# The order of the weights' loads, and the queue of some other transfers, in a hybrid decoder layer on one core

## The chip, the core and the metric

The kernel runs on one core of one Trainium2 chip. The core has engines that each work through their own list of instructions in order: TensorE (PE, with its weight loads shown apart as PEld), VectorE (DVE), ScalarE (ACT), GpSimd (POOL) and SyncE (SP). SP computes nothing here; it issues transfers between the chip's main memory and the core's own memory. ACT and POOL can issue transfers too, POOL as one of its ordinary instructions. The transfers of all of them are carried by the same 16 DMA engines. The metric is the device time of one execution in microseconds (us); a lower one is better.

## The reference

One inference step of a one-layer decoder is computed in float32, for a prompt of 2048 tokens and for a small batch of 8 samples with 4 tokens each. With the model width 1024:

```python
xn  = rms_norm(x, norm_mix_pre)
qk, v_m, o_m, gates, q_a, k_a, v_a = split(xn @ w_in)         # 1024 x 2312
c_new, h = mlstm(short_conv(qk), v_m, gates)                  # 4 heads, chunks of 128 tokens
att      = windowed_attention(q_a, k_a, v_a, sinks)           # 8 heads, window 128
y_m = sigmoid(o_m) * rms_norm(h, mlstm_norm);  y_a = rms_norm(att, attn_norm)
x = x + rms_norm([y_m, y_a] @ w_out, norm_mix_post)           # 1024 x 1024
u = rms_norm(x, norm_ffn_pre)
x = x + rms_norm(relu(u @ w_up)**2 @ w_down, norm_ffn_post)   # 1024 x 4096 x 1024
x = x + sigmoid(x @ w_pgate) * (p @ w_pproj)                  # 1024 x 1024 and 256 x 1024
```

The mLSTM head group keeps a running maximum `m` along the tokens (the stabiliser of its exponentials), so the weights of a chunk of 128 tokens are `exp(log_d - m_t)`, where `m_t` is one maximum for each head and token. Outputs are the tokens' `x` and the new states of both head groups.

## The kernel before

**Tiling and stages.** The prompt is cut into 16 blocks of 128 tokens. A first stage (`project`, called once for each of six chunks of two or three blocks) does the norm, the input projection and, interleaved with it, the mLSTM recurrence (`mlstm_chunk`) and the windowed attention (`swa_chunk`). The small batch goes with the last chunk. Both head groups write their results to a scratch tensor in main memory, `yd`, two halves of 512 columns for each block. Then three groups of two chunks go, one after another, through the output projection (`mix_load`, `mix_mm`, `mix_post`), the MLP (`mlp`, 16 steps of 256 hidden columns, of which the first two are plain and the others build the product `u @ w_up` from seven smaller ones) and the gated embedding (`gate_post`, `gate_embed`, `gate_mm`).

**Precision.** Each weight matrix piece is split into two parts, a rounded high part and the remainder, and each product is made of three matmuls (`mm3`). So a weight that is used for the first time is loaded as it is (a tile `wr`, or `wb` for the blocks of `w_up`), copied to the high part by ACT (line 254), and the remainder is made on POOL or DVE (line 255). The pair (a tile `w`, 528 KB or less) is then also stored to a scratch tensor `wk` in main memory, and later chunks load the finished pair from there.

**The ring of weights** (`Ring`). There are five raw tiles and seven pair tiles (`RAWS, PAIRS`, line 75), used in turn. A list (`plan`) gives the weights in the order in which TensorE uses them, and `take` makes the next one where the program reaches it: `get` takes a pair tile, stores an earlier pair that is due (`store`, line 282, on POOL), and either loads the kept pair (line 289) or calls the maker, which loads the raw weight and splits it. Raw loads stand in `product` (line 307, the `wb` blocks), `row` (351), `heads` (363), `multi` (374) and `pairs` (385). All of them are issued by `dma`, which is SP's queue; `put` is POOL's queue:

```python
dma, put = nc.sync.dma_start, nc.gpsimd.dma_start
here = tc.keep_in_program_order
```

**What sets the order.** The program text is not the order in which an engine gets its instructions. A planner in the framework lets a clock of its own run with estimated durations, and gives each engine the next instruction that by this clock is ready, so an instruction with nothing to wait for can be placed far ahead of its place in the text. On the chip each engine then keeps the planned order and waits at an instruction until its inputs are there. `here(ins)` takes away the planner's freedom for one instruction: it is placed behind the instruction that was written before it on the same engine, whichever that was. TensorE's instructions are all kept in the order of the text (class `Flow`). Of SP's transfers none is; of POOL's, the stores of pairs (line 282) and one store of the decode stage are.

**The other transfers on SP's queue** are the input blocks `x` (line 477), constants, the broadcast of the running maxima to all partitions (`weights` in `mlstm_chunk`, line 961, tile `Wt`, one for each of the 16 blocks; ACT stores the maxima to the scratch tensor `mbd` in line 906, and DVE adds a mask to `Wt` in line 962, an instruction that is kept in the order of the text), the two halves of `yd` for the output projection (`load_y`, line 848), the two post-norm weight vectors (`gain`, line 1453, tiles `gpost` and `gffn`, which use one buffer in turn), the rows of `p` (lines 1875 and 1877) and the last six stores of the output (`finish`, line 1833, where `last` is true for the chunk of blocks 14 and 15 and the small batch; each has two halves of 512 columns). All other output stores of line 1833 go over POOL.

Of the kernel before, what the change touches and what calls it, by code (L numbers as in the profile page):

```python
# [11 lines left out]
U32 = mybir.dt.uint32  # L12
# [6 lines left out]
P = 128  # L19
D = 1024  # L20
# [10 lines left out]
AD = 64  # L31
# [91 lines left out]
def bc(ap, axis, n):  # L123
    v = ap.unsqueeze(axis)
    shape = list(v.shape)
    shape[axis] = n
    return v.broadcast_to(tuple(shape))
# [71 lines left out]
def hybrid_layer(ctx: ExitStack, tc: tile.TileContext, A, O):  # L199
# [4 lines left out]
    dma, put = nc.sync.dma_start, nc.gpsimd.dma_start  # L204
    here = tc.keep_in_program_order
# [47 lines left out]
    def wsplit(hi, lo, src, eng=None):  # L253
        act.copy(hi, src)  # L254
        ins = (eng or weng()).tensor_tensor(lo, src, hi.bitcast(F32), ALU.subtract)  # L255
        if pinned:
            here(ins)

    class Ring:


# [22 lines left out]
        def get(self, key, n, make):  # L284

            t = self.tile(n)
            self.store()
            if key in self.kept:
                dma(t.bitcast(U32), self.kept[key])
            else:  # L290
                make(t[:, 0], t[:, 1])
                if self.uses[key] > 1:
                    self.keep(key, t)
            return t[:, 0], t[:, 1]
# [4 lines left out]
        def product(self, key, i, src):  # L299


            def make(h, l):
                if i == 0:
                    self.blocks = []
                    for e in range(2):
                        t = self.wide.tile([P, KT // 2, 2 * P], F32, tag="w", name=f"{self.nm}b{self.n}{e}")
                        dma(t, src[e * 512 : (e + 1) * 512].rearrange("(k p) n -> p k n", p=P))
                        self.blocks += [t[:, :, :P], t[:, :, P:]]
                a11, a21, a12, a22 = self.blocks
                eng = iter([dve if e == "d" else pool for e in UENG[i]])  # L310
                h, l = [v.rearrange("p (k n) -> p k n", k=4) for v in (h, l)]
                if i == 2:
                    next(eng).tensor_tensor(a21, a21, a22, ALU.add)
                    next(eng).tensor_tensor(a11, a21, a11, ALU.subtract)
                elif i == 3:
                    self.last = self.tile(512)
                    wsplit(*[self.last[:, e].rearrange("p (k n) -> p k n", k=4) for e in range(2)], a22, next(eng))
                    next(eng).tensor_tensor(a22, a22, a11, ALU.subtract)
                elif i == 6:
                    next(eng).tensor_tensor(a12, a12, a11, ALU.subtract)  # L320
                wsplit(h, l, (a11, a12, a11, a22, None, a21, a12)[i], next(eng))

            if i == 4 and key not in self.kept:
                t = self.last
                if self.uses[key] > 1:
                    self.keep(key, t)
                v = t[:, 0], t[:, 1]
            else:
                v = self.get(key, 512, make)
            return [t.rearrange("p (k n) -> p k n", k=4) for t in v]  # L330
# [17 lines left out]
        def row(self, key, src, n):  # L348
            def make(h, l):
                raw = self.load(n)  # L350
                dma(raw, src)
                wsplit(h, l, raw)

            return self.get(key, n, make)

        def heads(self, key, src, j, n):


            def make(h, l):
                raw = self.load(n)  # L360
                for s in range(2):
                    o = s * 256 + j * AD
                    dma(raw[s * AD : (s + 1) * AD], src[o : o + AD])
                wsplit(h, l, raw)

            return self.get(key, n, make)

        def multi(self, key, srcs, kn, n):
            three = lambda v: v.rearrange("p (k n) -> p k n", k=kn)

            def make(h, l):
                raw = self.load(kn * n)
                for off, w, s in srcs:
                    dma(three(raw)[:, :, off : off + w], s)
                wsplit(h, l, raw)

            return [three(v) for v in self.get(key, kn * n, make)]

        def pairs(self, key, segs):


            def make(h, l):
                raw = self.load(512)
                for s, src in enumerate(segs):
                    dma(raw.rearrange("p (k s n) -> p k s n", k=2, s=2)[:, :, s], src)
                v = raw.rearrange("p (k s j c) -> p k j s c", k=2, s=2, j=2)
                h, l = (t.rearrange("p (k j s c) -> p k j s c", k=2, j=2, s=2) for t in (h, l))
                for k in range(2):
                    wsplit(h[:, k], l[:, k], v[:, k])

            return [v.rearrange("p (k n) -> p k n", k=2) for v in self.get(key, 512, make)]
# [451 lines left out]
    def load_y(pool_, tag, b):  # L843

        src = yds if b == "s" else yd[b]
        t = pool_.tile([P, D], F32, tag=tag, name=f"y_{b}")
        for e in range(2):
            dma(t[: src[e].shape[0], e * 512 : e * 512 + 512], src[e])
        return t

    def mix_heads(x, i, b, t, banks=ps_m):
# [100 lines left out]
    def mlstm_chunk(r, blocks):  # L952
# [5 lines left out]

        def weights(i):
            Wt = sm.tile([P, MH, P], F32, tag="Wt", name=f"Wt{blocks[i]}")  # L960
            dma(Wt, bc(r["mbd"][:, i * P : (i + 1) * P], 0, P))
            here(dve.tensor_tensor(Wt, Wt, bc(mask, 1, MH), ALU.add))
            for h in range(MH):
                act.activation(Wt[:, h], Wt[:, h], AF.Exp, bias=cq(i, 0, h), scale=-1.0)
            Ws[i] = Wt
# [12 lines left out]
        for i, b in enumerate(blocks):  # L978
# [15 lines left out]
            Wt = Ws.pop(i)  # L994
# [40 lines left out]
        while todo:  # L1035
            finish()
            yield 0.5
# [412 lines left out]

    def gain(src, nm):
        g = gp.tile([P, D], F32, tag="g", name=nm)
        dma(g, src[0:1, :].broadcast_to((P, D)))
        return g

    gpost, gffn = gain(A["norm_mix_post"], "gpost0"), None
# [41 lines left out]
    f, yt, ut, xt = {}, {}, {}, {}  # L1498
# [126 lines left out]

    def mlp(gi, chunks, sample):
        nonlocal gffn
        gffn = gain(A["norm_ffn_post"], f"gffn{gi}")
        G = f"{gi}"
        if sample:  # L1630
            f["t"] = es2.enter_context(tc.tile_pool(name="ft", bufs=1, reuse_waits="tile")).tile(
# [3 lines left out]
        def up(s, ci, wu, hid):  # L1635
            c = chunks[ci]
            W = len(c) * P + (HS if sample else 0)
            x = ut[ci]
            for ft in range(FS):
                nm = f"{G}{s}{ci}{ft}"  # L1640
                fs_ = slice(ft * P, (ft + 1) * P)
                ps = psum(ps_mm, "up" + nm)
                for k in range(KT):
                    w = [t[:, k % 2, fs_] for t in wu[k // 2]]
                    mm3(ps[:, :W], w, x.at(k, slice(0, W)), k == 0, k == KT - 1)
                    pe.tick()
                t = wp.tile([P, UW], F32, tag="re", name="re" + nm)[:, :W]
                hidden(s, ci, ft, t, ps[:, :W], hid)
                pe.tick()
# [131 lines left out]
        def down_weights():  # L1781
            return [[t[:, :512] for t in w] for w in ring.take(FS)]
# [3 lines left out]
        for ci in range(2):  # L1786
            if ci == 1:
                pe.drain(tsp)
                pe.drain(dec)
                es_lp.close()  # L1790
                es_t = ExitStack()
                tp = es_t.enter_context(tc.tile_pool(name="tp", bufs=1, side="right", reuse_waits="tile"))
                ring.wide = es_t.enter_context(tc.tile_pool(name="wide", bufs=WIDE, side="right", reuse_waits="tile"))
                tsp.add(sums())
            for s in range(FAST):
                if ci == 0:
                    hids.append({})
                up(s, ci, ring.take(4), hids[s])
            for s in range(FAST):
                for half in range(2):  # L1800
                    down(s, ci, half, down_weights(), hids[s])
# [23 lines left out]
    def finish(b, half, pg, pv, n, nm, last):  # L1825
        hs = slice(half * 512, half * 512 + 512)
        t = gw.tile([P, 512], F32, tag="sg", name=f"sg{nm}{half}")
        act.activation(t[:n], pg, AF.Tanh, scale=0.5)
        dve.scalar_tensor_tensor(t[:n], t[:n], 1.0, pv, ALU.add, ALU.mult)
        o = gw.tile([P, 512], F32, tag="ot", name=f"ot{nm}{half}")  # L1830
        dve.scalar_tensor_tensor(o[:n], t[:n], 0.5, f[b][:n, hs], ALU.mult, ALU.add)
        dst = y_s[:, hs] if b == "s" else y_p[b * P : (b + 1) * P, hs]
        (dma if last else put)(dst, o[:n])

    def gate_post(gi, ci, c, sample):

# [168 lines left out]
```

## Time and profile before

| | |
|---|---|
| time, median of 3 runs | 2611.17 us (2611.08 to 2614.02) |
| the profiled execution, its own time | 2623.78 us |
| its span, from the first instruction to the last | 2621.7 us |
| mean granted TensorE clock in it | 0.989 of full speed |
| busy: PE, DVE, ACT, POOL | 2534.7, 1483.0, 974.3, 620.3 us |
| transfers: SP's queue (q1), POOL's queue (q0) | 474.02 MB, 174.54 MB |

The profile is of one execution, and that execution took 12.61 us more than the median of the runs. A row of the timeline or of the chain of waits begins with the start in us from the first instruction and the duration. An `SPq` row is an issue of a transfer by SP's queue; where several are merged into one row, the duration goes from the start of the first to the end of the last, waits between them included. Square brackets give the idle time of the engine just before the instruction and what ended it. A row of the list of waits reads: who waited, for whom, the sum in us, how many times, the longest. A row of the list of issues gives the count, the size and the median time from the issue to the landing. A row by stretch of time gives, for PE, PEld, DVE, ACT and POOL, the busy time and the number of instructions, and then the granted clock, the share of the DMA engines that was busy, and GB/s.

### The profile page before, as it was taken

The numbers are of one execution on the slowest core, as the hardware profiler recorded it, in microseconds if no ns is written. First come the engines' busy times: TensorE is split into PE (matmuls) and PEld (weight loads), VectorE is DVE, ScalarE is ACT, GpSimd is POOL, SyncE is SP. The second block draws the span as 40 slices with busy tenths as digits, with TensorE's granted clock in tenths as the row PEclk, the third lists the DMA queues.
The fourth block names the chain that finished last, engine by engine and source line by source line (L and its number), as shares of the span: only waits on it lengthen the run. The fifth ranks groups of instructions, "written<-read, shape, count | busy, mean of one in ns | idle before, by whom it ended". The sixth has DMA issues, their size and how long they took to land.

```text
span 2621.7 us, 39337 instructions
## 1 busy us (share of the span) xinstructions
PE 2534.7 (97%) x14260; PEld 2204.3 (84%) x14260; DVE 1483.0 (57%) x3162; ACT 974.3 (37%) x2167; POOL 620.3 (24%) x988
## 2 busy tenths in 40 slices
PE   7999999998999999999999999999999999999998
PEld 7787888777778888888877788999998879999986
DVE  6666656665657655656744654444446346444553
ACT  5545444544445444444523342222223134222231
POOL 5311111112433666666523200000001011000010
PEclk9999999999999999999999999999999999999999
DMA  9756656576898666666799765555556899777787
GB/s 315 273 192 201 207 181 213 194 244 227 260 343 287 254 250 253 244 254 251 271 341 318 255 201 188 188 191 188 187 187 233 295 334 359 253 255 256 256 299 235
DMA packets 220433, 651.10 MB, mean 248 GB/s; under 512 B 25397, under 2 KB 59401, under 8 KB 220224
## 3 DMA queue, kind: packets, MB, share of 16 engines
q1 hardware_dynamic: 170032, 474.02, 53.4%
q0 software_dynamic: 50160, 174.54, 17.3%
q8 instruction: 113, 1.85, 0.3%
q14 instruction: 80, 0.66, 0.1%
q10 hardware_dynamic: 48, 0.03, 0.0%
HBM read 494.34 MB, written 155.25 MB: 248 GB/s over the span
## 4 chain that ended last, share of the span: by engine, by line
PE 77%; DVE 8%; DMA 7%; issue 3%; ACT 2%; POOL 2%; SPq 0%; ACTq 0%; DVEq 0%; POOLq 0%
PE up L148 21%; PE dn L148 21%; PE mo L148 5%; PE pg L148 5%; PE v L148 3%; DMA w<-wk 3%; PE o L148 3%; DMA wk<-w 2%; PE qk L148 2%; PE qa L148 2%; PE gv L148 2%; DVE hl L232 2%; PE aT L152 1%; PE aO L148 1%; PE pv L148 1%
## 5 line engine op out<-in xcount | busy, mean ns | idle before, releaser
L148 PE MATMUL dn<-w,hh 128*128 128x512 f32 x1792 | 564.0, 396 | 6.3 <-ACT re L1654 3.8
L1759 DVE TENSOR_TENSOR f<-f,dn 128x512 f32<-128x512 f32 x420 | 286.9, 686 | 220.5 <-PE dn L148 218.4
L148 PEld LDWEIGHTS dn<-w,hh 128*128 128x128 f32 x1792 | 334.2, 189 | 84.7 <-DVE f L1759 6.8
L148 PE MATMUL dn<-w,hl 128*128 128x512 f32 x896 | 354.5, 396 | 1.6 <-DVE hl L232 1.6
L1734 DVE TENSOR_TENSOR re<-up,re 128x384 f32<-128x384 f32 (+1 forms) x294 | 151.9, 517 | 320.2 <-PE up L148 320.2
L148 PEld LDWEIGHTS dn<-w,hl 128*128 128x128 f32 x896 | 168.8, 188 | 43.5 <-DVE hl L232 5.1
L1735 ACT COPY re<-up 128x384 f32<-128x384 f32 (+1 forms) x42 | 18.8, 448 | 392.0 <-PE up L148 392.0
L1654 ACT ACTIVATE re<-re 128x384 f32<-128x384 f32 (+1 forms) x168 | 83.0, 494 | 207.5 <-DVE re L1734 203.9
L232 DVE TENSOR_TENSOR hl<-re,hh 128x384 fp32r<-128x384 f32 (+1 forms) x192 | 137.6, 717 | 16.8 <-ACT hh L231 15.7
L282 POOL DMA_DIRECT2D wk<-w x242 | 134.1, 556 | 34.4 <-DVE w L255 25.2
L254 ACT CAST w<-wr 128x512 fp32r<-128x512 f32 (+2 forms) x152 | 88.9, 597 | 95.9 <-PE up L148 32.3
L254 ACT CAST w<-wb 128x512 fp32r<-128x512 f32 x98 | 60.6, 620 | 168.4 <-PE dn L148 114.6
L255 POOL TENSOR_TENSOR w<-wr,w 128x512 fp32r<-128x512 f32 (+2 forms) x76 | 100.2, 1319 | 80.5 <-ACT w L254 79.5
L255 POOL TENSOR_TENSOR w<-wb,w 128x512 fp32r<-128x512 f32 x70 | 92.3, 1319 | 110.3 <-ACT w L254 109.8
L1460 POOL DMA_DIRECT2D x<-x1d x16 | 8.7, 545 | 463.5 <-PE up L148 449.4
L1655 ACT ACTIVATE re<-re 128x384 f32<-128x384 f32 (+1 forms) x192 | 94.9, 494 | 5.9
L231 ACT CAST hh<-re 128x384 fp32r<-128x384 f32 (+1 forms) x192 | 92.6, 482 | 8.3
L1067 ACT ACTIVATE s<-s,swt 128x257 f32<-128x257 f32 (+1 forms) x128 | 63.3, 496 | 65.8 <-DVE swt L1064 65.8
L1061 DVE CUSTOM_DVE_ANT_0 s<-aS,cst,sink 128x256 f32<-128x256 f32 (+1 forms) x128 | 57.1, 472 | 52.0 <-PE aS L148 51.6
L148 PE MATMUL up<-t2h,w 128*128 128x384 f32 (+1 forms) x336 | 85.1, 320 | 0.0
L148 PE MATMUL up<-t0h,w 128*128 128x384 f32 (+1 forms) x336 | 85.1, 320 | 0.0
L148 PE MATMUL up<-t1h,w 128*128 128x384 f32 (+1 forms) x336 | 85.1, 320 | 0.0
(1526 smaller groups left out, 6415.7 us busy)
## 6 DMA issues: line engine op xcount, KB each, us to landing
w<-wk SPq DMA_DIRECT2D x728, 512.0 KB, 4.9
wk<-w POOLq DMA_DIRECT2D x238, 512.0 KB, 7.2
wr<-in_w_down_dram SPq DMA_DIRECT2D x64, 256.0 KB, 8.2
wb<-in_w_up_dram SPq DMA_DIRECT2D x28, 512.0 KB, 6.9
w<-wk SPq DMA_DIRECT2D x20, 528.0 KB, 3.9
x<-in_x_prompt_dram SPq DMA_DIRECT2D x16, 512.0 KB, 4.4
y<-yd SPq DMA_DIRECT2D x32, 256.0 KB, 7.0
xr<-in_x_prompt_dram POOLq DMA_DIRECT2D x16, 512.0 KB, 9.4
```

Source lines behind the costliest of these rows:

```text
L148: ins = self.pe.matmul(out, lhsT, rhs, start=start, stop=stop)
L231: act.copy(hi, src)
L232: dve.tensor_tensor(lo, src, hi.bitcast(F32), ALU.subtract)
L254: act.copy(hi, src)
L255: ins = (eng or weng()).tensor_tensor(lo, src, hi.bitcast(F32), ALU.subtract)
L282: here(put(self.kept[key], t.bitcast(U32)))
L1061: dve.tensor_tensor_reduce(s_[:, s, lo : 2 * P], pS[:, s, lo:], bias[:, j, lo:], 1.0 if s == 0 else 0.0625, sink[:, h : h + 1], ALU.add, A ...
L1067: act.activation(e_, e_, AF.Exp, bias=nm[:, s : s + 1], accum_out=sm[:, s : s + 1])
L1654: act.activation(t, src, AF.Relu)
L1655: act.square(t, t)
L1734: add = lambda out, a, b: dve.tensor_tensor(out, a, b, ALU.add)
L1759: dve.tensor_tensor(out(i), out(i), ps, ALU.add)
```

## The change

A helper `wload` is added that issues a load on SP's queue and keeps it in the order of the text. All loads of weights (kept pairs and the five kinds of raw loads) use it. Five kinds of other transfers change in queue or place: the broadcast of the maxima, the two halves of `yd` and the post-norm weights go over POOL's queue; the `gffn` vector is loaded later in `mlp`, where the second chunk's part begins, instead of at its start; and of the last six stores the three of the first half go over POOL's queue, so that SP keeps three.

```diff
+    def wload(out, src):
+
+        here(dma(out, src))
+
...
             if key in self.kept:
-                dma(t.bitcast(U32), self.kept[key])
+                wload(t.bitcast(U32), self.kept[key])
...
-                        dma(t, src[e * 512 : (e + 1) * 512].rearrange("(k p) n -> p k n", p=P))
+                        wload(t, src[e * 512 : (e + 1) * 512].rearrange("(k p) n -> p k n", p=P))
...
-                dma(raw, src)
+                wload(raw, src)
...
-                    dma(raw[s * AD : (s + 1) * AD], src[o : o + AD])
+                    wload(raw[s * AD : (s + 1) * AD], src[o : o + AD])
...
-                    dma(three(raw)[:, :, off : off + w], s)
+                    wload(three(raw)[:, :, off : off + w], s)
...
-                    dma(raw.rearrange("p (k s n) -> p k s n", k=2, s=2)[:, :, s], src)
+                    wload(raw.rearrange("p (k s n) -> p k s n", k=2, s=2)[:, :, s], src)
...
         for e in range(2):
-            dma(t[: src[e].shape[0], e * 512 : e * 512 + 512], src[e])
+            put(t[: src[e].shape[0], e * 512 : e * 512 + 512], src[e])
...
             Wt = sm.tile([P, MH, P], F32, tag="Wt", name=f"Wt{blocks[i]}")
-            dma(Wt, bc(r["mbd"][:, i * P : (i + 1) * P], 0, P))
+            put(Wt, bc(r["mbd"][:, i * P : (i + 1) * P], 0, P))
...
         g = gp.tile([P, D], F32, tag="g", name=nm)
-        dma(g, src[0:1, :].broadcast_to((P, D)))
+        put(g, src[0:1, :].broadcast_to((P, D)))
...
     def mlp(gi, chunks, sample):
         nonlocal gffn
-        gffn = gain(A["norm_ffn_post"], f"gffn{gi}")
...
             if ci == 1:
                 pe.drain(tsp)
+                gffn = gain(A["norm_ffn_post"], f"gffn{gi}")
                 pe.drain(dec)
...
-        (dma if last else put)(dst, o[:n])
+        (dma if last and half == 1 else put)(dst, o[:n])
```

## The prediction

> **What bounds the kernel now.** I read the page's busy times first, then the list of waits of PE, then that of SP's queue, and then the timelines where the two meet.
>
> ```profile
> span 2621.7 us, 39337 instructions
> PE 2534.7 (97%) x14260; PEld 2204.3 (84%) x14260; DVE 1483.0 (57%) x3162; ACT 974.3 (37%) x2167; POOL 620.3 (24%) x988
> ```
>
> PE bounds it. The change takes no matmul away, so all it can win is PE's idle time, 2621.7 - 2534.7 = 87.0 us, and what idle time costs afterwards in clock. Of PE's waits, these name a kept weight (`w<-wk`), and one more will turn out to be for one:
>
> ```profile
> PE mo L148 <- DMA w<-wk: 5.5, 3, 2.8
> PE qk L148 <- DMA w<-wk: 4.5, 3, 3.9
> PE pg L148 <- DMA w<-wk: 1.8, 1, 1.8
> PE up L148 <- DMA w<-wk: 1.6, 1, 1.6
> ```
>
> That is 13.4 us, and with 3.7 us more (in Part 2) 17.1: 0.7% of the span is about the whole prize. On SP's queue the waits that stand ahead of weights without being about them are these (the second row is of the stretch 690 to 760 us, as is the third; the others are of the whole run):
>
> ```profile
> SPq L961 <- DMA mbd<-Mt: 33.1, 6, 7.0
> SPq L374 <- DVE w L255: 11.3, 1, 11.3
> SPq L289 <- DMA wk<-w: 6.6, 1, 6.6
> SPq L1833 <- DVE ot L1831: 12.6, 3, 10.9
> ```
>
> Most of these waits hurt nobody, because the ring holds seven pairs. The sum is made only where one of them meets a wait of PE.
>
> **Part 1: the maxima leave SP's queue.** In the last chunk SP came to line 961 after its weights, ACT had only then issued the store of the maxima, and SP stood until it landed. The weights behind it came late:
>
> ```profile
> 586.81 14.64 SPq L289 DMA_DIRECT2D w<-wk  x8
> 608.20 0.92 SPq L961 DMA_DIRECT2D Wt<-mbd  x2
> 609.22 30.63 SPq L289 DMA_DIRECT2D w<-wk  x13
> ...
> 602.43 0.25 ACTq L906 DMA_DIRECT2D mbd<-Mt  x1
> ...
> 614.84 0.58 PE L148 MATMUL qk<-x5h,w 128*128 128x256 f32 x1 [3.91 <-DMA w<-wk]
> ...
> 612.90:619.70 6.80, 4.86 (x23) 4.86 (x24) 1.81 (x4) 0.80 (x2) 0.18 (x1) 0.50 0.66 267
> ```
>
> SP stood from 586.81 + 14.64 = 601.45 to 608.20. PE lost 3.91 us, and then ran 4.86 busy us at a clock of 0.50, of which half, 2.43 us, is a loss: 6.3 us together. The load that PE waited for is the next one on SP, so with that wait gone it is issued up to 6.75 us earlier, more than PE's 3.91. The wait goes to POOL, and there it has room: POOL sat idle at just that time,
>
> ```profile
> 609.46 0.50 POOL L616 DMA_DIRECT2D zsd<-qa1se  x1 [8.17 <-DVE qa1se L570]
> ```
>
> so behind it stand a small store and copies that nobody wants soon. In the other places PE waited 4.5 - 3.9 = 0.6 us for `qk`'s weights, and I count that at the end. **Gain 6.3 us**, between 3.9 (if the clock falls for another reason) and 6.3.
>
> **Part 2: loads keep their turn.** At the change from the output projection to the MLP the planner had put raw loads of `w_up` (line 374) ahead of kept weights that PE needs sooner. Their raw tiles were not free, and SP stood:
>
> ```profile
> 701.00 14.38 SPq L374 DMA_DIRECT2D wr<-in_w_up_dram  x4
> 715.48 9.64 SPq L289 DMA_DIRECT2D w<-wk  x5
> ...
> 726.92 1.19 PE L148 MATMUL mo<-w,yt01h 128*128 128x512 f32 x2 [3.73 <-DVE ms L1490]
> ...
> 725.50:732.30 6.80, 5.38 (x13) 4.13 (x14) 4.54 (x11) 1.15 (x2) 4.41 (x9) 0.50 1.02 408
> ```
>
> For the kept weight issued at 715.48 the list of issues of that moment alone gives its time to landing, and so it does for the pair's store issued at 710.88:
>
> ```profile
> w<-wk SPq DMA_DIRECT2D x1, 512.0 KB, 11.3
> ...
> wk<-w POOLq DMA_DIRECT2D x1, 512.0 KB, 12.1
> ```
>
> 715.48 + 11.3 = 726.8, which is when PE went on: the page names DVE, but the weight ended this wait. Full price: 3.73 and half of 5.38, 6.4 us. But PE needs the second weight at once too, and its load waited the 6.6 us quoted above for a store of the pair that held its place in the ring, 710.88 + 12.1 = 723.0. That wait is POOL's and not SP's order; with it alone, and a load that then takes 5 us, PE would stand to about 728 again. The store took 12.1 us while DMA was full, partly of the 4 x 256 KB put ahead, which at the 408 GB/s of that stretch are 2.6 us. So the bounds are 0 and 6.4 and I take the row of those 2.6 us, rounded down: **gain 2 us**. The raw loads of `w_up` now start later, behind sixteen kept ones; three of the eight did so before with no wait of PE, so nothing for that. In the long stage of fresh `wb` blocks the order changes too (SP had them two steps ahead, now one). A step lasts 913.17 - 881.13 = 32.0 us, which covers a landing of 6.9 us:
>
> ```profile
> 881.13 2.74 SPq L307 DMA_DIRECT2D wb<-in_w_up_dram  x2
> ...
> 913.17 2.74 SPq L307 DMA_DIRECT2D wb<-in_w_up_dram  x2
> ...
> wb<-in_w_up_dram SPq DMA_DIRECT2D x28, 512.0 KB, 6.9
> ```
>
> **Part 3: the post-norm weights.** In the last group SP stood at `gffn` until DVE had done with `gpost`, with PE's next weight behind it:
>
> ```profile
> 2169.60 0.33 SPq L1453 DMA_DIRECT2D gffn<-in_norm_ffn_post_dram  x1
> 2170.02 3.97 SPq L289 DMA_DIRECT2D w<-wk  x5
> ...
> 2176.73 0.39 PE L148 MATMUL up<-ut20h,w 128*128 128x272 f32 x1 [1.57 <-DMA w<-wk]
> ```
>
> **Gain 1.6 us** (0 to 1.6: the DMA engines are full here). In its new place `gffn` is wanted only in the last of the sixteen steps of `mlp`.
>
> **Part 4: the halves of `yd` and the last stores.** 34 loads and three stores leave SP. No wait of PE stands behind them, also not behind the 10.9 us that SP waited for the last `ot`: **0**.
>
> **What POOL pays.** 16 + 34 + 6 + 3 = 59 more transfers, each as the 28 of line 1833:
>
> ```profile
> L1833 POOL DMA_DIRECT2D out_dram<-ot x28 | 15.3, 545 | 153.2 <-DVE ot L1831 153.2
> ...
> 661.61 0.53 POOL L616 DMA_DIRECT2D zsd<-vse  x1 [11.77 <-DVE vse L570]
> ...
> SPq L289 <- DMA wk<-w: 21.6, 7, 8.0
> ```
>
> 59 x 0.545 = 32 us, on an engine that is busy 24%. It is on the path in two places at most. Ahead of the output projection six halves and `gpost` (7 x 0.545 = 3.8 us) come before splits and stores of the first `w_out`; POOL had 11.77 idle us there. In the gated embedding of the first group six halves and `gpost` stand among stores of `w_pgate`, whose landing SP awaits in the stretch 1330 to 1365 us (the third row); PE's 1.8 us for `pg` are there. 0 to 3.8 each; I take 1 us each since POOL has gaps in both: **cost 2 us**.
>
> Sum: 6.3 + 2 + 1.6 - 2 = 7.9 us, made against the profiled 2623.78 (2615.9 then); the same off the median, 2611.17 - 7.9 = 2603.3, and with the 0.6 us of Part 1 **2602.7 us**.
>
> The Trainium skill, DMA: Bandwidth & Descriptors, section Issuing engines are not separate DMA queues, says that transfers of all issuers share the same 16 engines, and that spreading them saves only the issuer's time. By it alone the change would win nothing but SP's issue time, which is hidden. The trace has in 601.45 to 608.20 what that sentence leaves out, a wait of one issuer that holds back unrelated transfers; I give its outcome a chance below, as the second rival.
>
> **The rivals.**
>
> *All waits at SP's hand go.* If the stores in Part 2 land sooner as well, the full 6.4 counts, and the 1.99 us at 741 with the half-clock stretch behind it:
>
> ```profile
> 741.54 0.73 PE L148 MATMUL mo<-w,yt01h 128*128 128x512 f32 x2 [1.99 <-DMA w<-wk]
> ...
> 742.60:746.00 3.40, 3.40 (x13) 2.81 (x12) 0.28 (x2) 0.00 (x0) 0.00 (x0) 0.50 1.03 420
> ```
>
> 6.9 + 6.4 + 1.99 + 1.70 + 1.6 = 18.6 with no cost on POOL: 2592.6 us. Against it: the ring's stores are still POOL's.
>
> *Nothing is won.* PE's weights are held by the ring's stores and by full DMA engines (`wk<-w` 21.6 us in 35 us of the gate stage, share 1.02), POOL's extra 32 us makes those stores later by as much as SP gains; and where unkept loads of `x` or `p` stand between, a weight is kept behind those and not behind the last weight, so the turn holds only in part. 2611 us.
>
> *Slower: `Wt` comes too late over POOL.* DVE's mask addition (line 962) is kept in its place, so DVE, and PE behind it, stand if `Wt` is late. The loads of a third block have little time: one took 8.6 us and DVE waited, another was issued 10.6 us ahead:
>
> ```profile
> 118.36 1.20 SPq L961 DMA_DIRECT2D Wt<-mbd  x1
> 126.97 0.69 DVE L962 TENSOR_TENSOR Wt<-Wt,cst 128x512 f32<-128x512 f32 x1 [2.67 <-DMA Wt<-mbd]
> ...
> 239.82 0.37 SPq L961 DMA_DIRECT2D Wt<-mbd  x1
> 250.39 0.68 DVE L962 TENSOR_TENSOR Wt<-Wt,cst 128x512 f32<-128x512 f32 x1
> ...
> Wt<-mbd SPq DMA_DIRECT2D x16, 256.0 KB, 4.2
> POOL hist L768 <- ACT u L767: 101.6, 24, 11.5
> ```
>
> 10.6 - 4.2 = 6.4 us are free; it decides when POOL's queue delays `Wt` by more. POOL's longest wait in this stage, 11.5, would do it, by 5.1 us, in the third blocks of chunks 0 to 3: four times, 20.4 us, less the 7.9: 2623.7 us. Against it: the median wait in that row is about 101.6 / 24 = 4.2.
>
> The Trainium skill, SBUF — State Buffer, section SBUF: two separate sides, speaks against this change as well: a transfer from GpSimd can wait until a DVE copy gives back a port that GpSimd needs to write the descriptors, and it tells of 3100 ns in place of 620. By it `Wt` would come some 2.5 us later, an estimate from that page, which the 6.4 us cover, and the sum stays.
>
> **How the numbers follow.** 0.42 for the forecast (2597 to 2608 in itself), 0.20 for the larger gain, 0.23 for nothing won, 0.15 for slower. A measurement tells 0.2%, 5.2 us, from no change: under 2605.9 is faster, over 2616.4 slower. Faster: 0.42 x 0.85 + 0.20 + 0.04 = 0.60; slower 0.15 and 0.03 of the third case: 0.18; the rest 0.22. The range goes from below the larger gain to most of the slower case: 2588 to 2619.
>
> **What would show it.** Part 1: SP goes on with weights at 601 us, and neither the 3.91 nor the half clock after it is there. Part 2: no line 374 ahead of the kept `w_out` pairs, and the wait before `mo` is under 3.7 us but not zero. Part 3: no 1.57 us at the start of the last `up`. POOL busy about 652 us. The forecast is wrong if DVE waits for `Wt` in line 962 for more than 10 us, if ACT's or SP's waits for `wk<-w` grow, or if the planner, given a new order on SP and POOL, moves work of DVE and ACT so that PE waits in places that this text doesn't name.

## The result, and the profile after

The kernel after took 2629.73 us (median of 4 runs, 2623.86 to 2632.42) against 2612.6 for the kernel before on the same chip: ratio 1.0063, 95% interval 1.0050 to 1.0075, about 16 us slower. The forecast was 2602.7, faster; the range went to 2619. **The direction was wrong.**

The page after, first its busy times, then rows of the list of PE's waits:

```profile
span 2630.6 us, 39303 instructions
PE 2534.9 (96%) x14260; PEld 2202.7 (84%) x14260; DVE 1476.7 (56%) x3162; ACT 973.8 (37%) x2167; POOL 651.2 (25%) x1047
```

```profile
PE mo L148 <- DMA w<-wk: 8.9, 7, 4.6
...
PE dn L148 <- ACT re L1657: 4.2, 1, 4.2
PE ut100t L152 <- DVE g L238: 3.3, 1, 3.3
PE yt5t L152 <- DVE g L238: 2.9, 1, 2.9
PE xt20t L152 <- DVE xt00l L232: 2.6, 1, 2.6
...
PE pg L148 <- DMA w<-wk: 2.2, 1, 2.2
PE up L148 <- DMA w<-wk: 1.3, 2, 1.1
PE qk L148 <- DMA w<-wk: 1.0, 2, 0.8
```

PE's work is the same; only its idle time grew. POOL's 651.2 us are the 31 us more that were forecast. Of the waits for kept weights, that of `qk` fell from 4.5 to 1.0 us; `up` has 1.3 instead of 1.6, `pg` 2.2 instead of 1.8, and `mo` 8.9 instead of 5.5, or instead of 9.2 if the 3.73 us that were for a weight, though labelled DVE, are counted with it. Of the waits for DVE shown here, `ut100t` had 1.5 us before, `yt5t` 1.1 and `xt20t` 0.8. The wait of `dn` for ACT's relu (`re`) moved: before had one too, of nearly the same size, but in the first MLP, where the kernel after has none. The row of the list, and of the timeline, before:

```profile
PE dn L148 <- ACT re L1654: 3.8, 1, 3.8
...
795.52 1.22 PE L148 MATMUL dn<-w,hh 128*128 128x512 f32 x2 [3.83 <-ACT re L1654]
```

The lines of the kernel after are 3 or 4 higher than those of before (the relu of `hidden` is L1654 before and L1657 after), and every load kept in turn now has line 261.

Where the two profiled executions part is seen from the start of the same matmul or transpose in both timelines (us from the start, rounded; the differences are of the times as recorded):

| first instruction of | stage | before | after | difference |
|---|---|---|---|---|
| `spqk` | last chunk, after Part 1's place | 621.6 | 612.1 | -9.4 |
| `ut00t` | output projection of group 0 done | 737.8 | 735.5 | -2.3 |
| `pt0t` | MLP of group 0 done | 1289.1 | 1280.1 | -9.0 |
| `ut110t` | start of the MLP of group 1 | 1505.5 | 1504.7 | -0.8 |
| `pt6t` | MLP of group 1 nearly done | 2010.2 | 2017.7 | +7.6 |
| `ut150t` | start of the MLP of group 2 | 2181.5 | 2190.8 | +9.3 |

So the gain was there at 612 us and was given back in three places: in the output projection of group 0 (+7.1), from the end of the first MLP to the start of the second (+8.2), and within the second MLP (+8.4). Between the first two of them, in the first MLP, the kernel after won 6.7 us again: the wait at 795.52 is gone there. So one such wait went and another came. The profiled execution of before was 12.6 us above the median of its runs, that of after 2.7, so the table shows the change some 10 us too well; it is read for places, and the medians of the experiments give the sizes.

**The place of the second MLP** is the clearest. In the plain steps of `mlp`, ACT's relu empties an accumulator of `up`, and `dn` needs the place. ACT before, then ACT and PE after:

```profile
1558.90 0.49 ACT L1654 ACTIVATE re<-up 128x384 f32<-128x384 f32 x1 [1.84 <-PE up L148]
```

```profile
1559.96 0.49 ACT L1657 ACTIVATE re<-up 128x384 f32<-128x384 f32 x1
1560.48 0.53 ACT L1658 ACTIVATE re<-re 128x384 f32<-128x384 f32 x1
1561.04 0.52 ACT L231 CAST hh<-re 128x384 fp32r<-128x384 f32 x1
1563.16 0.83 ACT L1703 CAST t2h<-ts 128x768 fp32r<-128x768 f32 x1 [1.61 <-DVE ts L1698]
1565.42 0.83 ACT L1719 CAST ut11h<-tl 128x768 fp32r<-128x768 f32 x1 [1.43 <-DVE tl L1718]
1566.16 0.48 ACT L1657 ACTIVATE re<-up 128x384 f32<-128x384 f32 x1
...
1566.70 0.88 PE L148 MATMUL dn<-w,hh 128*128 128x512 f32 x2 [4.24 <-ACT re L1657]
```

```profile
1567.10:1570.50 3.40, 3.40 (x10) 2.62 (x9) 3.14 (x4) 1.78 (x5) 0.00 (x0) 0.50 0.38 122
```

Before, the relu ran as soon as PE had finished `up`. After, two casts of the operand sums of the later steps (`t2h`, `ut11h`) stand ahead of it in ACT's list, and each waits for DVE. PE starts 0.06 us after the relu's end, 4.24 us late, and runs 3.4 us at half clock (last row: 0.50). No row here waits for a weight or for POOL. What changed is the order of ACT's and DVE's lists.

**The places that the forecast named.** Part 1's wait is gone: SP issues one weight after another and waits only for PE to free places in the ring; PE has 2.01 us at `qa` left (before: 0.96). The slower rival's wait of DVE for `Wt` (second of the next two fences, from the answer on line 966, the mask addition) is 0.7 us in all, once:

```profile
581.21 58.61 SPq L261 DMA_DIRECT2D w<-wk  x24
...
597.84 0.58 PE L148 MATMUL qa<-x5h,w 128*128 128x256 f32 x1 [2.01 <-DMA w<-wk]
```

```profile
  DMA Wt<-mbd: 0.7, 1
```

Part 2's order is as forecast too, no raw load of `w_up` ahead of kept `w_out` pairs, and yet `mo` waits more in this stage than before, 7.9 us between 710 and 760 us where it was 5.7:

```profile
708.29 28.75 SPq L261 DMA_DIRECT2D w<-wk  x11
...
719.70 0.70 PE L148 MATMUL mo<-w,yt01h 128*128 128x512 f32 x2 [2.00 <-DMA w<-wk]
725.19 1.22 PE L148 MATMUL mo<-w,yt01h 128*128 128x512 f32 x2 [4.57 <-DMA w<-wk]
```

Part 3's wait is still there, 1.12 us instead of 1.57, with no `gffn` on SP:

```profile
2187.62 0.40 PE L148 MATMUL up<-ut20h,w 128*128 128x272 f32 x1 [1.12 <-DMA w<-wk]
```

### The profile page after: what moved, and what is told of

Same layout as the page of the kernel before. It is cut to its first block, busy times and chain, and to the rows that moved or that the text cites. A ratio compares the mean times of both kernels' runs of the same rounds, so it can differ in the third digit from the quotient of the medians.

```text
span 2630.6 us, 39303 instructions
## 1 busy us (share of the span) xinstructions
PE 2534.9 (96%) x14260; PEld 2202.7 (84%) x14260; DVE 1476.7 (56%) x3162; ACT 973.8 (37%) x2167; POOL 651.2 (25%) x1047
## 5 line engine op out<-in xcount | busy, mean ns | idle before, releaser
L1657 ACT ACTIVATE re<-re 128x384 f32<-128x384 f32 (+1 forms) x168 | 83.3, 496 | 202.4 <-DVE re L1737 199.0
L232 DVE TENSOR_TENSOR hl<-re,hh 128x384 fp32r<-128x384 f32 (+1 forms) x192 | 115.1, 599 | 18.2 <-ACT hh L231 17.0
L255 DVE TENSOR_TENSOR w<-wr,w 128x512 fp32r<-128x512 f32 (+2 forms) x76 | 72.6, 961 | 29.5 <-ACT w L254 27.6
L1666 POOL COPY hs<-hh 128x16 f32<-128x16 f32 x32 | 10.5, 327 | 305.8 <-ACT hh L231 305.8
```

What stands on the lines that cost most here:

```text
L232: dve.tensor_tensor(lo, src, hi.bitcast(F32), ALU.subtract)
L1657: act.activation(t, src, AF.Relu)
```

## The experiments

Three theories: **A**, the kept turn changes the planned order of DVE and ACT, and PE waits there; **B**, POOL's 59 more transfers delay what others wait for; later **D**, of these only the halves of `yd` do so. Ratios are to the kernel before, run alongside (medians 2609.7 to 2610.5 us), with 95% intervals; 0.001 is 2.6 us. Diffs are against the kernel before unless another is named. Line numbers in experiments are those of the kernel after, or up to 2 higher, except that loads not kept in turn have their own.

### The turn alone, and everything but the turn

```diff
# e1: all six loads of weights, nothing else
-                dma(t.bitcast(U32), self.kept[key])
+                wload(t.bitcast(U32), self.kept[key])
...
# e2: the kernel after with these six as dma(...) again
```

> The kernel before, with only the weights' loads kept in their turn; all other transfers stay on SP's queue. Theory A (the loss is made where PE waits for DVE and ACT, because keeping the loads in turn changes the planned order of these two engines): the waits of the profile after at 1291.95 and 1295.85 (1.77 and 2.65 us, transposes of xt), at 1499.47 (3.29, transposes of ut) and at 1566.70 (4.24, dn waits for ACT's re) are here too, the stretches 1280-1310, 1490-1510 and 1550-1571 lose 5, 3 and 7 us, and nothing of the 9 us that the kernel after had won by 615 us is guaranteed: 2620 to 2630 us. Theory B (POOL's 59 more transfers delay what DVE and SP wait for): 2605 to 2613, no slower than before.

> The kernel after, with the weights' loads left to the planner as before; maxima, mix halves, post-norm weights and first halves of the last stores on POOL. Theory A: the waits at 1291.95, 1295.85, 1499.47 and 1566.70 go, about 15 us back: 2603 to 2615 us. Theory B: as slow as after, 2625 to 2632 us.

Measured: e1 2652.6 us, ratio 1.0164 (1.0150 to 1.0178); e2 2618.41 us, 1.0025 (1.0014 to 1.0036). B alone falls: with nothing new on POOL the turn costs 42 us. A alone falls as well: e2 lies above A's range and below B's, so the loss has a part without the turn, and e1 lost more than A asked for. Most of that rest is a third mechanism, seen in the timeline of e1 (SP, then PE):

```profile
1464.79 0.32 SPq L261 DMA_DIRECT2D w<-wk  x1
1486.57 0.33 SPq L1457 DMA_DIRECT2D gffn<-in_norm_ffn_post_dram  x1
1487.32 4.06 SPq L261 DMA_DIRECT2D w<-wk  x7
...
1493.45 0.66 PE L148 MATMUL up<-ut10h,w 128*128 128x384 f32 x1 [12.89 <-DVE rq L1523]
```

A load kept in turn is placed behind whatever was written before it on SP. Here that is `gffn`, which waits for DVE's last use of `gpost`, and 21 us pass without a load. (The wait is labelled DVE, but the load issued at 1487.32 takes 6.0 us to land in the list of issues of that moment, which is 1493.3.) Waits of 9.5 us at 763.82 and 8.1 us at 2619.56 stand behind `gffn` and the last stores in the same way. In the kernel after these others are on POOL, so that part of the cost is absent. But e2 is 1.0025 and the kernel after 1.0063: the turn costs about 10 us there too.

### Which loads' turn, and is it DVE's and ACT's order

```diff
# e7: the kernel after, kept pairs free
-                wload(t.bitcast(U32), self.kept[key])
+                dma(t.bitcast(U32), self.kept[key])
# e8: the kernel after, the five raw loads free, kept pairs in turn
# e9: the kernel after, and in sums():
-                eng.tensor_tensor(t1, b12[0], b11[0], ALU.subtract)
+                ins = eng.tensor_tensor(t1, b12[0], b11[0], ALU.subtract)
+                if gi == 1:
+                    here(ins)
```

> The kernel after, but only the raw loads keep their turn; the kept pairs (line 293) are left to the planner. Theory A: DVE's and ACT's planned order in 1450-1600 us is that of before again, so the waits at 1499 (3.29) and 1566 (4.24, dn for ACT's re) go; those at 1292 and 1296 (xt) stay: 9 to 12 us less than after, 2617 to 2621 us. Rival (the turn costs by weights that land late, wherever they are): the waits of DVE and ACT stay or the time falls by under 4 us, 2625 to 2631.

> The kernel after, but only the loads of kept pairs keep their turn; the raw loads are left to the planner. Theory A: the waits of xt at 1292 and 1296 go, 4 to 6 us less than after; the waits at 1499 and 1566 stay: 2622 to 2627 us. Rival (weights that land late): raw loads of w_up stand ahead of kept w_out pairs again as in the profile before, and a wait of mo over 3 us is back at 715-730: 2630 us or more.

> The kernel after, in which one instruction more keeps its place: in the second group, the first subtraction of each half of the operand sums (line 1686 of the kernel after). SP's and POOL's queues have the order of the kernel after throughout; on ACT the relu of the plain steps stands ahead of the casts of the sums again, nearly as before. Theory A (the kept loads cost through DVE's and ACT's planned order in the sums): the waits at 1554.82 (0.89) and 1566.70 (4.24) and half clock behind them go, 5 to 9 us less than the kernel after, which was 1.0063 of before: ratio 1.003 to 1.0045. Rival (the kept loads land later in their turn, and this is what costs): the ratio stays at 1.006 or above.

Measured: e7 2612.03 us, 1.0006 (0.9995 to 1.0017); e8 2632.47 us, 1.0086 (1.0069 to 1.0102); e9 2616.31 us, 1.0030 (1.0019 to 1.0040). The turn of the kept pairs is the larger loss (e8 against e2, 0.0061, 16 us); the raw loads' turn gives some 5 us back beside it (e7 against e2, intervals that just touch). Two of these missed what A expected: e7 is 5 us faster, and e8 lies in the range of the rival, late weights, though the wait of over 3 us at `mo` that the rival asked for is not in its trace (2.68 us is the longest). e9 decides between A and late weights: the same loads in the same turn, one instruction of DVE held in place in each half, and 0.0033, 8.6 us, come back. PE in 1540 to 1600 us, after and then e9:

```profile
1540.00:1600.00 60.00, 54.78 (x275) 49.45 (x274) 37.88 (x53) 24.38 (x45) 1.11 (x2) 0.97 0.61 208
```

```profile
1540.00:1600.00 60.00, 60.00 (x297) 53.60 (x296) 43.80 (x61) 21.44 (x38) 0.00 (x0) 1.00 0.64 219
```

PE's first number after the stretch is its busy time: 5.2 us of idle are gone, and the clock is 1.00 throughout. With half of the 3.4 us at half clock that is 6.9 of the 8.6 us. So this loss is shown to be the order of DVE and ACT, and not a weight. The other traces agree: the wait of `dn` in the second MLP, 4.2 to 4.5 us, stands in the four that keep the kept pairs in turn without this hold (after, e1, e8, e12) and in none of the other thirteen.

The rest of the 16 us is not settled by a run. One more place is seen: PE's wait for DVE at `ut100t`, at the start of the same group, is 2.8 to 3.3 us in after, e8, e9 and e12, and 1.4 to 1.5 wherever the kept pairs are free (in e1, which stood 12.89 us shortly before it, there is none). The raw loads' turn has a place of its own, `xt20t`, in the second of the three places of the table: 1.7 to 5.4 us with it, 0.8 without.

### The other parts, each alone

```diff
# e3
-            dma(Wt, bc(r["mbd"][:, i * P : (i + 1) * P], 0, P))
+            put(Wt, bc(r["mbd"][:, i * P : (i + 1) * P], 0, P))
# e4: gain() by put, gffn at its later place
# e15
-        (dma if last else put)(dst, o[:n])
+        (dma if last and half == 1 else put)(dst, o[:n])
# e5
-            dma(t[: src[e].shape[0], e * 512 : e * 512 + 512], src[e])
+            put(t[: src[e].shape[0], e * 512 : e * 512 + 512], src[e])
```

> The kernel before, with only the broadcast of the maxima moved to POOL's queue. Theory A, in which Part 1 of the prediction stands (the profile after was 9.4 us ahead at 615 us): the wait of 3.91 us at 614.84 and the half clock behind it go, and nothing is lost later: 2602 to 2607 us. Theory B: 2610 to 2614. The slower rival of the prediction (the maxima come too late over POOL): above 2615.

> The kernel before, with only the post-norm weights moved to POOL's queue and the later place of gffn in the text. Theory A: the planned order moves only a little around 750-850, 1500 and 2150-2200 us: 1.6 us won at the start of the last up, some 1.5 lost before ut130t, 2608 to 2615 us. Theory B: the post-norm weights wait on POOL for DVE, with the powers of the norm behind them (in the profile after, gffn waited 1.69 us at 1492.41 with two powers behind it), in all three groups, 2615 to 2622 us.

> The kernel before, with only the first halves of the last six stores over POOL's queue; DVE's and ACT's planned order is unchanged throughout. The prediction's Part 4 counts them at nothing: ratio 0.999 to 1.001. If the end of the run waits for a store that POOL issues later: 1.001 to 1.002.

> The kernel before, with only the halves of yd loaded over POOL's queue. Everything but the turn cost 8 us although the maxima alone won 5 and the post-norm weights alone 3. Theory D (the six halves of a group stand in POOL's queue where splits and stores of w_out and w_pgate were, so the kept weights come late in the stretches 700-740 and 1300-1400 us): 2618 to 2627 us, with waits of mo and pg for kept weights of more than 2 us. Theory E (the parts don't add up: each new planned order is another draw): 2606 to 2614.

| part alone | median, us | ratio | in us |
|---|---|---|---|
| e3, maxima | 2605.31 | 0.9978 (0.9969 to 0.9987) | -5.7 |
| e4, post-norm weights | 2607.38 | 0.9989 (0.9981 to 0.9998) | -2.9 |
| e15, last stores | 2610.05 | 1.0003 (0.9995 to 1.0012) | +0.8, none that can be told |
| e5, halves of `yd` | 2622.29 | 1.0051 (1.0035 to 1.0066) | +13.3 |

The four add up to 5.5 us, and all four together (e2) measured 6.5. Theory D holds: one kind of transfer, counted at nothing, outweighs the gains of two others; that the parts add up speaks against theory E. e4 does not win where it was to win: the wait at the start of the last `up` is 1.97 us in its trace. What its trace lacks is the wait of `dn` for ACT's relu in the first MLP, 3.83 us in before. It is 2.9 to 3.9 us in the seven traces that have `gffn` on SP and no turn (before, e3, e5, e11, e13, e14, e15), and gone in all nine with `gffn` on POOL. So that is likely the gain; no run tests it alone, and why ACT's order changes there stays open.

### Where the halves cost

```diff
# e13; e14 has the condition the other way round
-            dma(t[: src[e].shape[0], e * 512 : e * 512 + 512], src[e])
+            (put if b != "s" and b < 6 else dma)(t[: src[e].shape[0], e * 512 : e * 512 + 512], src[e])
# e11: e5, and in sample_evac
-            put(zsd[:, zoff + o : zoff + o + w], t)
+            dma(zsd[:, zoff + o : zoff + o + w], t)
```

> The kernel before, with only the halves of yd of the first group (blocks 0 to 5, twelve transfers) over POOL's queue. If the cost of the halves (ratio 1.0051 for all) is made where POOL's work for fresh weights of w_out stands behind them, in 600-740 us: 1.003 to 1.005. If each group pays its share, as in the later stages of the profile with the halves alone (waits at 1361 and 1433): 1.001 to 1.002.

> The kernel before, with only the halves of yd of the second and third group and of the sample (22 transfers) over POOL's queue. DVE's and ACT's planned order is that of before but for four places. If the cost is in the first group: 0.999 to 1.001. If each group pays its share: 1.003 to 1.004.

> The kernel before, with the halves of yd over POOL's queue and the sample's stores to zsd (line 620) over SP's. With the halves alone on POOL (ratio 1.0051) POOL stood 10.17 us at 675.98 for DVE's ose, with the splits and stores of w_out behind it. If that standing is the cost of the halves in this stage: POOL goes on at 665, the waits of mo for kept weights at 717 and 735 (1.47 and 5.95) fall to under 3 together, and the ratio falls by 0.002 to 0.004, to 1.001 to 1.003. If the six issues themselves cost it, or the halves' landing: no change, 1.004 to 1.006.

Measured: e13 2616.31 us, 1.0027 (1.0017 to 1.0037); e14 2609.18 us, 1.0003 (0.9992 to 1.0013); e11 2616.15 us, 1.0033 (1.0020 to 1.0047). What can be placed of the cost sits in the first group; the 22 later transfers are free by themselves. (e13 and e14 together are 0.0030, less than e5's 0.0051; the intervals allow that they are equal, and the other 0.0021 is not placed.) POOL's timeline, with the halves on SP (e6, below), and then in e13:

```profile
657.39 1.31 POOL L255 TENSOR_TENSOR w<-wr,w 128x512 fp32r<-128x512 f32 x1
659.05 1.35 POOL L255 TENSOR_TENSOR w<-wr,w 128x512 fp32r<-128x512 f32 x1 [0.35 <-ACT w L254]
660.34 1.09 POOL L286 DMA_DIRECT2D wk<-w  x2
664.85 1.29 POOL L255 TENSOR_TENSOR w<-wr,w 128x512 fp32r<-128x512 f32 x1 [3.42 <-ACT w L254]
666.09 0.56 POOL L286 DMA_DIRECT2D wk<-w  x1
672.27 0.53 POOL L620 DMA_DIRECT2D zsd<-ose  x1 [5.62 <-DVE ose L574]
```

```profile
660.58 1.29 POOL L255 TENSOR_TENSOR w<-wr,w 128x512 fp32r<-128x512 f32 x1 [0.21 <-ACT w L254]
661.82 3.25 POOL L852 DMA_DIRECT2D y<-yd  x6
665.05 0.54 POOL L286 DMA_DIRECT2D wk<-w  x1
675.79 0.52 POOL L620 DMA_DIRECT2D zsd<-ose  x1 [10.19 <-DVE ose L574]
676.32 1.86 POOL L255 TENSOR_TENSOR w<-wr,w 128x512 fp32r<-128x512 f32 x1
...
723.20 0.73 PE L148 MATMUL mo<-w,yt01h 128*128 128x512 f32 x2 [3.00 <-DMA w<-wk]
...
737.70 1.22 PE L148 MATMUL mo<-w,yt01h 128*128 128x512 f32 x2 [5.41 <-DMA w<-wk]
```

The six halves take only 3.25 us of POOL, but they also push two splits and their stores behind POOL's next wait, the store of `ose`, which then stands for 10.19 us with nothing to do. Splits and stores of `w_out` begin again at 676 instead of going on at 659. Fifty us later the kept pairs of `w_out`, whose loads need these stores and their ring places, are late for `mo`; that the chain runs through these stores is read from the order of the rows. e11 took `zsd` away from POOL: POOL did go on with its splits at 667.89, only to stand 10.30 us for another result of DVE at 682.87. The ratio fell by 0.0018, but `mo` waited 4.46 and 1.61 us in its trace, not the under 3 that was expected, and the intervals of e5 and e11 overlap. So POOL's standing is seen, and is likely part of the cost; that it is all of it is not shown.

### Combinations

```diff
# e6: maxima, post-norm weights, last stores on POOL; no turn, halves on SP
# e10: e6, with the five raw loads as wload(...)
# e12: the kernel after with
-            put(t[: src[e].shape[0], e * 512 : e * 512 + 512], src[e])
+            dma(t[: src[e].shape[0], e * 512 : e * 512 + 512], src[e])
```

> The kernel after without the kept turn and with the halves of yd back on SP's queue: maxima, post-norm weights and first halves of the last stores on POOL. Theory D: the gains of the maxima and of the post-norm weights add up, 5 + 3 us: 2600 to 2605 us, below both kernels. Theory E: 2608 to 2618.

> Maxima, post-norm weights and first halves of the last stores on POOL as in the kernel after, the raw loads in their turn, but kept pairs left to the planner and the halves of yd on SP's queue. If the turn of the raw loads is a gain by itself (with the halves on POOL it went from ratio 1.0025 to 1.0006, some 6 us), it adds to the 0.9976 without a turn: 2596 to 2601 us, ratio 0.9945 to 0.9965. If it only mended what the halves on POOL had spoiled (raw loads of w_up ahead of kept w_out pairs): ratio 0.997 to 1.000.

> The kernel after with only the halves of yd back on SP's queue (all loads of weights in their turn). If the halves cost the same here as without the turn (12 us): 2615 to 2620 us, ratio 1.002 to 1.004. If the weights, which are kept behind the transfer written before them, now stand behind halves that wait for their buffers (in the kernel with the turn alone, whose halves were on SP too, first waits of 9.5, 12.9 and 8.1 us stood on PE): ratio above 1.006.

Measured: e6 2603.8 us, 0.9976 (0.9964 to 0.9988); e10 2604.86 us, 0.9978 (0.9968 to 0.9989); e12 2614.11 us, 1.0019 (1.0008 to 1.0030). e6 is faster than both kernels: the change without its two costly parts. So is e3 with one edit, and the two can't be told apart. e10, which gives the raw loads their turn on top of e6, adds nothing: it seems that the raw loads' turn only mends what the halves had spoiled. e12 gives back 0.0044, 11.5 us: the halves cost in the turn what they cost without it.

## Why the prediction was wrong

None of the rivals happened as told. The nearest is "nothing is won", which has POOL's stores come later, but holds that loss down to what SP gains.

**Part 1 (6.3 us, 3.9 to 6.3): right.** e3 won 5.7 us (3.4 to 8.1). That the size fits so well is in part luck: it was read from one execution, and in the six other traces with the maxima on SP and no turn (e4, e5, e11, e13, e14, e15) the wait of `qk` is 2.1 to 2.9 us, not 3.91. The slower rival, `Wt` late over POOL, did not happen: 0.7 us on DVE. By the sentence on the port in the Trainium skill, SBUF — State Buffer, section SBUF: two separate sides, such transfers would come later. The median landing of `Wt` did go from 4.2 to 5.9 us, 1.7 where the estimate from the page was 2.5, while that of the halves went the other way, from 7.0 to 5.0; so no run here shows the port as the reason, and the 6.4 us of room covered it as said. (The 4.2 us that the text calls the median wait of POOL, 101.6 / 24, are the mean.)

**Part 2 (2 us, 0 to 6.4): this step failed.** The order at 701 to 715 us became what was forecast. Its effect there is small and not shown as a gain in time: with the halves on SP, `mo` waits 2.7 and 3.2 us in all between 710 and 760 us where the loads keep their turn (e1, e12), 3.5 with the raw loads' turn alone (e10), and 3.7 to 5.7 without a turn (before, e3, e4, e6, e14, e15); that is 0.5 to 3 us, near the 2 forecast, but e10 was no faster than e6. What failed is the bound below. It was set at 0 because the text looked only for what SP's order does to SP's loads, and dismissed "the order changes too" in the `wb` stage as covered by a step of 32 us. But the planner orders DVE and ACT by the same clock as SP. Keeping the kept pairs in turn changed their lists in the second MLP, half a run away. That cost 8.6 us by e9, and the turn of the kept pairs 16 us in all (e8 against e2); where the other half goes is open but for `ut100t`. The forecast's last sentence names this very mechanism as what would make it wrong, without a price or a chance.

**Part 3 (1.6 us, 0 to 1.6): the reason was wrong, and that the size was near is luck.** e4 won 2.9 us (0.5 to 5.0), but the wait of 1.57 us at the last `up` remained at 1.12 after and 1.97 in e4: the weight there was not late because of `gffn`. The gain seems to lie in the first MLP, which the text does not name. In the second group, `gffn` took its wait with it to POOL: it stood 1.69 us at 1492.41, with two powers of the norm at 1493.65 behind it.

```profile
1492.41 0.61 POOL L1457 DMA_DIRECT2D gffn<-in_norm_ffn_post_dram  x1 [1.69 <-DVE f L1472]
1493.08 0.56 POOL L1518 DMA_DIRECT2D x1d<-f  x1
1493.65 1.08 POOL L1495 TENSOR_TENSOR ms<-ms,nhalf 128x1 f32<-128x1 f32 x2
```

This is at the start of that group's MLP, not where its second chunk's part was written: the later place in the text moved nothing.

**Part 4 and what POOL pays (0, and 2 us): this step failed, too.** The stores cost nothing (e15). The halves cost 13.3 us (9.1 to 17.2). The price of the issues was right, 3.25 us for six; what was missing is what those 3.25 us push behind the next wait in POOL's list. The text put "POOL had 11.77 idle us there" down as room, but idle time in front of an instruction that is in turn is no room for what stands behind it. "No wait of PE stands behind them" was true of SP's list, where the halves came from, and was asked of the wrong queue.

So the sum of -7.9 should have read -5.7 (maxima) -2.9 (post-norm weights) +13.3 (halves) +10 (the turn, once the others are off SP): 14.7 of the 16 us measured. This is a weak test, since the 10 is itself what the kernel after has above e2; what it tests is that the first three add up to e2, 4.7 where 6.5 was measured. The Trainium skill, DMA: Bandwidth & Descriptors, section Issuing engines are not separate DMA queues, has it that another issuer saves only the issuer's time. Neither e3 nor e5 agrees: the same kind of move, of 16 and of 34 transfers, gave -5.7 and +13.3 us, through what stood behind each in an issuer's list, as far as the rows above show it.

## What to carry to other kernels

Moving a transfer to another queue has two sides: what it no longer holds back, and what it pushes behind the next wait of the list that it joins. Idle time of the new issuer is room only behind its wait, not in front of it. Where a planner orders all engines by one clock, an edit on one queue can reorder others far away, so each kind of edit should be timed alone: here two of five won, and together with the rest they lost. A load that is kept in program order inherits every wait written before it on its queue (e1: 30.5 us in three waits of PE).

## What the runs showed that was not expected

The half-clock time at a wait came in lengths of 3.4, 6.8 and 10.2 us (the last from 720.7 us on in the kernel after, at its wait of 4.57 us), and once of 13.65 us. In e1 a wait of 12.89 us was followed by, and partly stood within, the longest one (row: start and end, length, PE's busy time and so on, the clock of 0.50):

```profile
1484.70:1498.35 13.65, 4.70 (x13) 3.89 (x14) 6.29 (x18) 3.45 (x6) 3.27 (x6) 0.50 0.90 304
```

So the price of a wait isn't proportional to its length: in the kernel after, waits of 2.01 us (at 597.84) and of 4.24 us (at 1566.70) were both followed by 3.4 us at half clock. And single profiled executions of one kernel differ by as much as these parts are worth: the one of before was 2623.78 us beside a median of 2611, which is why places were read from traces here and sizes from medians. Much of that is clock: its mean granted clock was 0.989, that of the profiled execution of e15, which plans DVE and ACT as before does, 0.994, and e15's took 2605.35 us. By an estimate from these figures, 0.005 of 2610 us, or 13 of the 18.4 us between them, is clock.
